# Low parts of the weights in three buffers, an own single buffer for the modulation vectors' tiles, and the mixer's parameters loaded later, in a hybrid diffusion layer on one core

## The chip, the cores and the metric

The kernel runs on one core of a Trainium2 chip. The time is that of the device in microseconds (us); the time before is the median of three runs. Engines are named as in the profile: PE is TensorE's matmul side and PEld its weight loads, DVE is VectorE, ACT is ScalarE, POOL is GpSimd, and SP is SyncE, whose queue (SPq) issues all of this kernel's DMAs. Every engine takes its instructions in the order in which the program lists them; an instruction that waits for a semaphore holds back all that is listed behind it on the same engine.

## The reference

One layer over 256 latent tokens and 256 context tokens of width 2048, in float32. Two conditioning vectors (`c` and `c_ctx`) give six modulation vectors each; the latent tokens use all six, the context tokens only the first two.

```python
mod = (silu_c @ w_mod[l] + b_mod[l])[:, None, :]
sh1, sc1, g1, sh2, sc2, g2 = jnp.split(mod, N_MOD, axis=-1)
h = modulate(rms_norm(x, norm_w[l, 0]), sh1, sc1)          # the same for ctx: hc
y, yc = token_mixers(h, hc, w_in[l], ..., w_out[l], ctx_out)
x = x + g1 * rms_norm(y, norm_w[l, 1])
h2 = modulate(rms_norm(x, norm_w[l, 2]), sh2, sc2)
x = x + g2 * rms_norm(conv_ffn(h2, ffn_up[l], ffn_conv_w[l], ffn_conv_b[l], ffn_down[l], True),
                      norm_w[l, 3])
```

`token_mixers` projects with `w_in` into seven parts, runs a gated linear recurrence in eight heads in both directions beside a convolution of width 31, and projects the two results with `w_out`. `conv_ffn` projects up to 2 x 5632 columns, convolves the gate half 3x3 on a grid, multiplies `gelu(gate)` with the other half and projects down.

## The kernel before

Every weight matrix is streamed through SBUF in tiles of 128 x 2048 float32 (1 MB). For full precision each tile is split: ACT casts it to the high part `whi` (L137), DVE subtracts to get the low part `wlo` (L140), and PE makes three products in place of one (high x high, high x low, low x high; L197 to L199 and L206 to L208). The raw tile is `raw`. Weight tiles are numbered here in the order in which they are used: 0 to 39 are five per head (ff, fb, q, b, a), 40 to 47 are g, 48 to 63 the output projection, 64 to 151 the up projection (gate and val in turn), 152 to 195 the down projection.

Four modulation vectors of the latent tokens (numbers 2 to 5 of the code) are not made on PE. Each is a sum over 16 tiles `graw` of 1 MB. DVE multiplies a tile with a column of the conditioning vector and adds it into an accumulator (L711 for the first tile of a vector, L713 for the others, two halves of 1024 columns a tile). Then `mod_cols` turns the accumulator by four groups of PE transposes `gT` (L727), and ACT sums them into columns (L730). The vector tiles are numbered 0 to 63 here: 0 to 15 are vector 2, 16 to 31 vector 3, 32 to 47 vector 4, 48 to 63 vector 5. One accumulator (`big`) serves vectors 2, 3 and 4.

The stages are: `phase0` (norm, first two modulation vectors, v projection), eight heads with `head_gemm` and `conv_gemm`, the g projections, `phase2` (output projection, residual, second norm), `phase3` (up projection with the grid convolution) and `phase4` (down projection). From the first head on, weight tiles are prepared ahead of their matmuls (`take`, `stage`).

What sets the order: a scheduler lists the instructions of each engine by readiness and priority. PE is held to the order of the code from the heads on (`self.order({ET.PE})`), so the place of the `gT` transposes between the matmuls is fixed by the code: `gemv` issues a vector's tiles at fixed places, and a count of PE time (`tick`) places the transposes about 5 us of matmuls behind the last tile. Splits of weight tiles have a raised priority (600), the sums of vector tiles a lowered one in the heads (-1000, `gemv_prio`) and none from the end of the heads on. Buffers come from pools: a tag with n buffers is a ring, in which tile k waits until tile k - n has been read for the last time. Before the change the rings are `raw` 3, `whi` 3 and `wlo` 2, and a vector tile takes its turn in the ring `raw` among the weight tiles, so that a weight tile can be loaded only when the vector tile ahead of it in the ring has been summed up. All DMAs stand in one queue on SP.

Of the kernel before, what the change touches and what calls it, by code (L numbers as in the profile page):

```python
# [8 lines left out]
F32 = mybir.dt.float32  # L9
# [6 lines left out]
P = 128  # L16
# [41 lines left out]
    ("lnw", HEADS),  # L58
    ("lnb", HEADS),
    ("hgw", 1),  # L60
    ("fcw", NFF * 9),
    ("fcb", NFF),
]
_POFF = {}
_n = 0
for _name, _w in _PCOLS:
    _POFF[_name] = (_n, _n + _w)
    _n += _w
NPAR = _n


def _ap(t, off, dims):
# [41 lines left out]
class _Kernel:  # L114
# [15 lines left out]
    def wtile(self, i, prio=600, hi=None, lo=None):  # L130

        src, (oh, ol) = self.srcs[i], self.places[i]
        raw = self.raws.pop(0) if self.raws else self.raw_tile(src, prio)
        with self.tc.high_priority(prio):
            if hi is None:
                hi = self.stg.tile([P, WBUF], F32R, tag="whi", name="whi", bufs=3)[:, oh:oh + 2048]
            self.nc.scalar.copy(hi, raw)  # L137
            if lo is None:
                lo = self.stg.tile([P, WBUF], F32R, tag="wlo", name="wlo", bufs=2)[:, ol:ol + 2048]
            self.nc.vector.tensor_sub(lo, raw, hi.bitcast(F32))  # L140
        return hi, lo

# [79 lines left out]

    def par(self, name, i=0, n=1):
        o = _POFF[name][0]
        return self.params[:, o + i:o + i + n]

    def rsqrt(self, out, t):

# [12 lines left out]
    def run(self):  # L241
# [90 lines left out]
        self.hid_hi = hid.tile([P, NFF, SEQ], F32R, name="hid_hi")  # L332
        self.hid_lo = hid.tile([P, NFF, SEQ], F32R, name="hid_lo")
        upp, up = enter(name="up", bufs=2, side="right")
        self.phase3(up)
        leave(upp)
        leave(h2p)
# [11 lines left out]
    def consts(self):  # L349
        nc, a, cst = self.nc, self.a, self.cst  # L350
        self.params = cst.tile([P, NPAR], F32, name="params")
        nc.sync.dma_start(self.params, a["params"])
        self.ident = cst.tile([P, P], F32, name="ident")
        self.masks = cst.tile([P, 5, 32], U8, name="masks")
        self.onecol = cst.tile([P, 1], F32, name="onecol")
        nc.gpsimd.memset(self.onecol, 1.0)
        self.mhalf = cst.tile([P, 2], F32, name="mhalf")
        nc.gpsimd.memset(self.mhalf, -0.5)


# [24 lines left out]
        self.oml = cst.tile([P, n], F32, name="oml")  # L385
        nc.vector.tensor_scalar(self.oml, self.lb, -1.0, 1.0, op0=ALU.mult, op1=ALU.add)


        o = _POFF["cT"][0]
        cc = self.params[:, o:o + 2 * KB]  # L390
        self.cs = cst.tile([P, 2 * KB], F32, name="cs")
        nc.scalar.activation(self.cs, cc, AF.Sigmoid)
        nc.vector.tensor_mul(self.cs, cc, self.cs)

        self.bsc1 = cst.tile([P, KB], F32, name="bsc1")
        nc.vector.tensor_scalar_add(self.bsc1, self.par("bmod", KB, KB), 1.0)
        self.ab = cst.tile([P, 2, KB, 2], F32, name="ab")
        self.mc = cst.tile([P, 4, KB], F32, name="mc")

    def late_consts(self):  # L400
        self.nc.sync.dma_start(self.ident, self.a["ident"])
# [9 lines left out]
    def phase0(self, p0, px, srcs):  # L411
# [49 lines left out]
        def gemv_row(q, t):  # L461

            if t == 0:
                rows[q] = px.tile([P, 512], F32, tag="row", name="row", bufs=P0_ROW)
            tag, n = (("raw", 3), ("whi", 3), ("wlo", 2), ("raw", 3), ("whi", 3), ("wlo", 2), ("raw", 3), ("whi", 3))[self.nt % 8]
            self.nt += 1
            w = self.stg.tile([P, 2048 if tag == "raw" else WBUF], F32, tag=tag, name="mraw", bufs=n)[:, 0:2048]
            nc.sync.dma_start(w, a["wm1"][q, t])
            for g in range(4):
                nc.tensor.matmul(rows[q][g * 32:(g + 1) * 32, :], cz[:, t * 4 + g, :], w[:, g * 512:(g + 1) * 512],  # L470
# [228 lines left out]

    def gemv_tile(self, s, kb):  # L700
        nc = self.nc
        w = self.stg.tile([P, 2048], F32, tag="raw", name="graw", bufs=3)
        nc.sync.dma_start(w, self.a["wm2"][s - 2, kb])
        c = self.cs[:, kb:kb + 1]
        if kb == 0:
# [524 lines left out]
def _pack(inputs):  # L1230
# [25 lines left out]
        "fcw": inputs["ffn_conv_w"][0].reshape(9, NFF, P).transpose(2, 1, 0).reshape(P, -1),  # L1256
        "fcb": _cols(inputs["ffn_conv_b"][0]),
    }
    a["params"] = np.ascontiguousarray(np.concatenate([parts[n] for n, _ in _PCOLS], axis=1))
    i = np.arange(P)  # L1260
    a["ident"] = np.eye(P, dtype=np.float32)
    a["masks"] = np.ascontiguousarray(np.stack(
# [3 lines left out]


# [11 lines left out]
```

## Time and profile before

| what | before |
|---|---|
| median of three runs | 1421.55 us (1419.74 to 1441.67) |
| profiled execution | 1419.87 us, of which the span from first to last instruction is 1418.1 us |
| PE busy | 1375.5 us (97%) |
| DVE busy | 1073.3 us (76%) |
| ACT busy | 716.6 us (51%) |
| DMA | 329.38 MB, mean 232 GB/s |
| mean granted TensorE clock | 0.995 |

Busy time is the time in which an engine had at least one instruction under way. Of the span, PE was idle for 1418.1 - 1375.5 = 42.6 us. A row of the timeline gives start, length, engine, line, operation, tiles and count, and in brackets the idle time ahead of it with what ended it. A row of the waits gives the sum in us, how many there were and the longest.

### The profile page before, as it was taken

The numbers are of one execution on the slowest core, as the hardware profiler recorded it, in microseconds if no ns is written. First come the engines' busy times: TensorE is split into PE (matmuls) and PEld (weight loads), VectorE is DVE, ScalarE is ACT, GpSimd is POOL, SyncE is SP. The second block draws the span as 40 slices with busy tenths as digits, with TensorE's granted clock in tenths as the row PEclk, the third lists the DMA queues.
The fourth block names the chain that finished last, engine by engine and source line by source line (L and its number), as shares of the span: only waits on it lengthen the run. The fifth ranks groups of instructions, "written<-read, shape, count | busy, mean of one in ns | idle before, by whom it ended". The sixth has DMA issues, their size and how long they took to land.

```text
span 1418.1 us, 24793 instructions
## 1 busy us (share of the span) xinstructions
PE 1375.5 (97%) x10272; PEld 1224.9 (86%) x10272; DVE 1073.3 (76%) x1577; ACT 716.6 (51%) x1174; POOL 31.2 (2%) x57
## 2 busy tenths in 40 slices
PE   4999999999999999999999999999999999999997
PEld 2566888888888898988999999999999998888886
DVE  4444788999999899777788788778878886767544
ACT  4333456666656665536744444454545443333532
POOL 0000001001000011000000000000000000000000
PEclk9999999999999999999999999999999999999999
DMA  9988676446645565788355555555555558878652
GB/s 374 391 325 330 258 267 218 160 188 238 222 167 207 208 226 189 286 305 302 123 205 180 205 185 203 181 206 189 199 184 203 193 194 340 312 287 306 242 187 106
DMA packets 49153, 329.38 MB, mean 232 GB/s; under 512 B 5392, under 2 KB 5648, under 8 KB 10896
## 3 DMA queue, kind: packets, MB, share of 16 engines
q1 hardware_dynamic: 49040, 327.80, 62.7%
q8 instruction: 80, 1.31, 0.4%
q14 instruction: 33, 0.27, 0.1%
HBM read 323.58 MB, written 4.19 MB: 231 GB/s over the span
## 4 chain that ended last, share of the span: by engine, by line
PE 77%; DVE 11%; ACT 4%; DMA 3%; issue 2%; POOL 2%; SPq 0%; DVEq 0%; POOLq 0%; ACTq 0%
PE val L197 6%; PE val L199 6%; PE val L198 6%; PE dn L206 6%; PE gate L197 6%; PE dn L208 6%; PE gate L199 5%; PE dn L207 5%; PE gate L198 5%; DVE wlo L140 3%; DVE acc L930 3%; PE v L206 2%; PE wo L208 2%; PE wo L206 2%; PE wo L207 2%
## 5 line engine op out<-in xcount | busy, mean ns | idle before, releaser
L137 ACT CAST whi<-raw 128x2048 fp32r<-128x2048 f32 x193 | 368.9, 1912 | 371.3 <-PE val L198 120.1
L140 DVE TENSOR_TENSOR wlo<-raw,whi 128x2048 fp32r<-128x2048 f32 x193 | 441.9, 2289 | 149.4 <-PE dn L207 59.7
L199 PE MATMUL val<-h,wlo 128*128 128x256 f32 x704 | 194.3, 276 | 0.0
L197 PE MATMUL val<-h,whi 128*128 128x256 f32 x704 | 194.3, 276 | 0.0
L198 PE MATMUL val<-h,whi 128*128 128x256 f32 x704 | 194.3, 276 | 0.0
L197 PE MATMUL gate<-h,whi 128*128 128x256 f32 x688 | 189.9, 276 | 0.0
L198 PE MATMUL gate<-h,whi 128*128 128x256 f32 x688 | 189.9, 276 | 0.0
L199 PE MATMUL gate<-h,wlo 128*128 128x256 f32 x688 | 189.9, 276 | 0.0
L1139 DVE SCALAR_TENSOR_TENSOR gacc<-gate,params,gacc 128x189 f32<-128x189 f32 (+2 forms) x352 | 152.4, 433 | 23.3 <-ACT gacc L1133 12.5
L206 PE MATMUL dn<-whi,hid_hi 128*128 128x512 f32 x352 | 137.4, 390 | 0.0
L208 PE MATMUL dn<-whi,hid_lo 128*128 128x512 f32 x352 | 137.0, 389 | 0.0
L207 PE MATMUL dn<-wlo,hid_hi 128*128 128x512 f32 x352 | 136.9, 389 | 0.0
L197 PEld LDWEIGHTS val<-h,whi 128*128 128x128 f32 x704 | 132.2, 188 | 0.0
L198 PEld LDWEIGHTS val<-h,whi 128*128 128x128 f32 x704 | 132.2, 188 | 0.0
L199 PEld LDWEIGHTS val<-h,wlo 128*128 128x128 f32 x704 | 132.1, 188 | 0.0
L199 PEld LDWEIGHTS gate<-h,wlo 128*128 128x128 f32 x688 | 129.2, 188 | 0.0
L197 PEld LDWEIGHTS gate<-h,whi 128*128 128x128 f32 x688 | 129.1, 188 | 0.0
L198 PEld LDWEIGHTS gate<-h,whi 128*128 128x128 f32 x688 | 129.1, 188 | 0.0
L713 DVE SCALAR_TENSOR_TENSOR big<-graw,cs,big 128x1024 f32<-128x1024 f32 x90 | 113.5, 1278 | 14.0 <-DMA graw<-in_wm_dram 13.9
L930 DVE SCALAR_TENSOR_TENSOR acc<-u,params,acc 128x242 f32<-128x242 f32 (+14 forms) x240 | 98.8, 472 | 0.0
L208 PEld LDWEIGHTS dn<-whi,hid_lo 128*128 128x128 f32 x352 | 66.1, 188 | 13.9
L207 PEld LDWEIGHTS dn<-wlo,hid_hi 128*128 128x128 f32 x352 | 66.1, 188 | 13.5
(270 smaller groups left out, 2681.4 us busy)
## 6 DMA issues: line engine op xcount, KB each, us to landing
raw<-in_wup_dram SPq DMA_DIRECT2D x88, 1024.0 KB, 4.8
graw<-in_wm_dram SPq DMA_DIRECT2D x64, 1024.0 KB, 5.0
raw<-in_win_dram SPq DMA_DIRECT2D x48, 1024.0 KB, 5.0
raw<-in_wdn_dram SPq DMA_DIRECT2D x44, 1024.0 KB, 4.9
mraw<-in_wm_dram SPq DMA_DIRECT2D x32, 1024.0 KB, 9.6
raw<-in_wout_dram SPq DMA_DIRECT2D x16, 1024.0 KB, 4.9
vraw<-in_wv_dram SPq DMA_DIRECT2D x16, 512.0 KB, 6.2
x<-in_x_dram SPq DMA_DIRECT2D x2, 1024.0 KB, 7.1
```

Source lines behind the costliest of these rows:

```text
L137: self.nc.scalar.copy(hi, raw)
L140: self.nc.vector.tensor_sub(lo, raw, hi.bitcast(F32))
L197: nc.tensor.matmul(out, wh, xh, start=start, stop=False)
L198: nc.tensor.matmul(out, wh, xl, start=False, stop=False)
L199: nc.tensor.matmul(out, wl, xh, start=False, stop=stop)
L206: nc.tensor.matmul(out, xh, wh, start=start, stop=False)
L207: nc.tensor.matmul(out, xh, wl, start=False, stop=False)
L208: nc.tensor.matmul(out, xl, wh, start=False, stop=stop)
L713: nc.vector.scalar_tensor_tensor(self.gacc[:, sl], w[:, sl], c, self.gacc[:, sl], op0=ALU.mult, op1=ALU.add)
L930: nc.vector.scalar_tensor_tensor(d, u[:, lo + o:hi + o], self.par("cw", j * CONVW + k), d, op0=ALU.mult, op1=ALU.add)
L1139: nc.vector.scalar_tensor_tensor(o, g[:, r0 + dy:r1 + dy, c0 + dx:c1 + dx], self.par("fcw", j * 9 + (dy + 1) * 3 + dx + 1), o, op0=ALU.mul ...
```

## The change

Three things are edited. The ring `wlo` has three buffers in place of two. Vector tiles `graw` no longer take their turn in the ring `raw`; they have a ring of their own with one buffer. The tiles `mraw` of the first stage, which go round the rings of the stream that is not yet running, use the ten buffers of all four rings. Room comes from a smaller scratch for DMA descriptors, and from the parameters: those of the grid convolution (`fcw`, `fcb`, 440 of the 921 columns) become a tensor of their own, `fparams`, which is loaded at the start of `phase3`. A tile `pad` of 56 columns that nothing uses is put behind the constants.

```diff
@@ parameters
+]
+
+_FCOLS = [
     ("fcw", NFF * 9),
     ("fcb", NFF),
 ]
@@ wtile
-                lo = self.stg.tile([P, WBUF], F32R, tag="wlo", name="wlo", bufs=2)[:, ol:ol + 2048]
+                lo = self.stg.tile([P, WBUF], F32R, tag="wlo", name="wlo", bufs=3)[:, ol:ol + 2048]
@@ par
         o = _POFF[name][0]
-        return self.params[:, o + i:o + i + n]
+        t = self.fparams if name in ("fcw", "fcb") else self.params
+        return t[:, o + i:o + i + n]
@@ run, ahead of phase3
         upp, up = enter(name="up", bufs=2, side="right")
+        self.fparams = up.tile([P, NFCP], F32, name="fparams", bufs=1)
+        nc.sync.dma_start(self.fparams, a["fparams"])
         self.phase3(up)
@@ consts
+        cst.tile([P, 56], F32, name="pad")
@@ gemv_row
-            tag, n = (("raw", 3), ("whi", 3), ("wlo", 2), ("raw", 3), ("whi", 3), ("wlo", 2), ("raw", 3), ("whi", 3))[self.nt % 8]
+            tag, n = (("raw", 3), ("whi", 3), ("wlo", 3), ("raw", 3), ("whi", 3), ("wlo", 3), ("graw", 1), ("raw", 3),
+                      ("whi", 3), ("wlo", 3))[self.nt % 10]
@@ gemv_tile
-        w = self.stg.tile([P, 2048], F32, tag="raw", name="graw", bufs=3)
+        w = self.stg.tile([P, 2048], F32, tag="graw", name="graw", bufs=1)
         nc.sync.dma_start(w, self.a["wm2"][s - 2, kb])
@@ kernel
-    nc = bacc.Bacc("TRN2", target_bir_lowering=False, num_devices=1)
+    nc = bacc.Bacc("TRN2", target_bir_lowering=False, num_devices=1, dynamic_dma_scratch_size=1024)
```

The lines of the kernel move by 5 to 12: L140, L703, L713, L727 before are L145, L714, L724, L738 after. PE's rows stay in the same order from end to end. Those of DVE and SP move, since the scheduler orders them by when buffers come free. The rows below leave out nothing between the first and the last of each piece; `x11` means that the row stands eleven times in a row.

The first place is DVE in the third head, around the end of the convolution of the head before it, where the sum of vector 2 ends. `acc` is the convolution's accumulator, `big` that of the vector, `ss` belongs to the readout. Before:

```order
L930 SCALAR_TENSOR_TENSOR acc<-u,params,acc 128x241
L933 TENSOR_TENSOR acc<-acc 128x256
L711 TENSOR_SCALAR big_101<-graw,cs 128x1024
L713 SCALAR_TENSOR_TENSOR big_101<-graw,cs,big_101 128x1024
L898 TENSOR_SCALAR ss<-ss 128x2
L140 TENSOR_TENSOR wlo<-raw,whi 128x2048
```

After:

```order
L941 SCALAR_TENSOR_TENSOR acc<-u,params,acc 128x241
L724 SCALAR_TENSOR_TENSOR big_102<-graw,cs,big_102 128x1024
L944 TENSOR_TENSOR acc<-acc 128x256
L724 SCALAR_TENSOR_TENSOR big_102<-graw,cs,big_102 128x1024 x11
L722 TENSOR_SCALAR big_102<-graw,cs 128x1024
L909 TENSOR_SCALAR ss<-ss 128x2
L145 TENSOR_TENSOR wlo<-raw,whi 128x2048
```

Before, all 16 tiles of vector 2 are summed ahead of this place, and the next row that reads `graw` (L711) opens vector 3. After, the halves of tile 10 stand around the row L944, and those of tiles 11 to 15 behind it in one block. At the same place in the sixth head, where vector 3 ends, the block has nine rows: the second half of tile 27 and tiles 28 to 31.

The second is SP's queue at the same place. Before, weight tile 7 to weight tile 14:

```order
L127 DMA raw<-in_win_dram 128x2048 x2
L703 DMA graw<-in_wm_dram 128x2048
L127 DMA raw<-in_win_dram 128x2048
L703 DMA graw<-in_wm_dram 128x2048
L127 DMA raw<-in_win_dram 128x2048 x2
L703 DMA graw<-in_wm_dram 128x2048
L127 DMA raw<-in_win_dram 128x2048 x2
L703 DMA graw<-in_wm_dram 128x2048 x2
L127 DMA raw<-in_win_dram 128x2048
```

After, weight tile 12 to weight tile 17:

```order
L132 DMA raw<-in_win_dram 128x2048
L714 DMA graw<-in_wm_dram 128x2048
L132 DMA raw<-in_win_dram 128x2048 x2
L714 DMA graw<-in_wm_dram 128x2048
L132 DMA raw<-in_win_dram 128x2048 x2
L714 DMA graw<-in_wm_dram 128x2048 x6
L132 DMA raw<-in_win_dram 128x2048
```

Before, vector tile 15, the last of vector 2, is issued between weight tiles 11 and 12. After, it is the fifth of the six that stand between weight tiles 16 and 17. Vector tile 10 is the one ahead of weight tiles 15 and 16.

The third place is DVE near the end of `phase2`, where vector 4 ends. `h` and `wroom` are rooms for low parts that lie outside the ring, `Y` and `part` belong to the residual, and L732 and L743 are the first rows that read the finished columns. Before:

```order
L713 SCALAR_TENSOR_TENSOR big_101<-graw,cs,big_101 128x1024 x2
L140 TENSOR_TENSOR h_6190<-raw,h_6190 128x2048 x2
L1007 TENSOR_TENSOR Y<-wo,G 128x512 x2
L1027 TENSOR_REDUCE part_6643<-ss_6199 128x2
L140 TENSOR_TENSOR wlo<-raw,whi 128x2048
L1028 TENSOR_SCALAR part_6643<-part_6643 128x2
L140 TENSOR_TENSOR wroom<-raw,wroom 128x2048
L140 TENSOR_TENSOR wlo<-raw,whi 128x2048
L732 TENSOR_TENSOR mc<-mc,params 128x16
```

After:

```order
L145 TENSOR_TENSOR wroom<-raw,wroom 128x2048
L1018 TENSOR_TENSOR Y<-wo,G 128x512 x2
L1038 TENSOR_REDUCE part_6644<-ss_6200 128x2
L145 TENSOR_TENSOR wlo<-raw,whi 128x2048
L1039 TENSOR_SCALAR part_6644<-part_6644 128x2
L145 TENSOR_TENSOR wlo<-raw,whi 128x2048
L724 SCALAR_TENSOR_TENSOR big_102<-graw,cs,big_102 128x1024 x4
L743 TENSOR_TENSOR mc<-mc,params 128x16
```

Before, vector tile 47 is summed ahead of the rows `Y` (the first row of the piece). After, tiles 46 and 47 are summed behind them and behind weight tiles 64 and 65; in SP's queue tile 46 stands behind weight tile 66 and tile 47 behind weight tile 68. In `phase4`, where vector 5 ends, the last two halves (tile 63) stand behind the low part of weight tile 181 before, and behind that of weight tile 184 after.

More of the change, by code (lines that the diff above doesn't have):

```diff
@@ L64 @@
 _POFF = {}
[L65 to L69, printed above, removed]
+for _list in (_PCOLS, _FCOLS):
+    _n = 0
+    for _name, _w in _list:
+        _POFF[_name] = (_n, _n + _w)
+        _n += _w
+NPAR = sum(_w for _, _w in _PCOLS)
+NFCP = sum(_w for _, _w in _FCOLS)
 def _ap(t, off, dims):
@@ L464, in gemv_row @@
                 rows[q] = px.tile([P, 512], F32, tag="row", name="row", bufs=P0_ROW)
-            tag, n = (("raw", 3), ("whi", 3), ("wlo", 2), ("raw", 3), ("whi", 3), ("wlo", 2), ("raw", 3), ("whi", 3))[self.nt % 8]
+            tag, n = (("raw", 3), ("whi", 3), ("wlo", 3), ("raw", 3), ("whi", 3), ("wlo", 3), ("graw", 1), ("raw", 3),
+                      ("whi", 3), ("wlo", 3))[self.nt % 10]
             self.nt += 1
-            w = self.stg.tile([P, 2048 if tag == "raw" else WBUF], F32, tag=tag, name="mraw", bufs=n)[:, 0:2048]
+            w = self.stg.tile([P, WBUF if tag[0] == "w" else 2048], F32, tag=tag, name="mraw", bufs=n)[:, 0:2048]
             nc.sync.dma_start(w, a["wm1"][q, t])
@@ L1258, in _pack @@
     }
-    a["params"] = np.ascontiguousarray(np.concatenate([parts[n] for n, _ in _PCOLS], axis=1))
+    for name, cols in (("params", _PCOLS), ("fparams", _FCOLS)):
+        a[name] = np.ascontiguousarray(np.concatenate([parts[n] for n, _ in cols], axis=1))
     i = np.arange(P)
```

## The prediction

> **What bounds the kernel now.** First the page's line of busy times, then a table of the stages, cut where PE's matmuls change name (first stage to 158.9, heads and g to 586.4, output projection to 688.3, up projection to 1167.3, down projection with vector 5 to 1344.9, and the rest), and PEld's waits for low parts.
>
> ```profile
> span 1418.1 us, 24793 instructions
> PE 1375.5 (97%) x10272; PEld 1224.9 (86%) x10272; DVE 1073.3 (76%) x1577; ACT 716.6 (51%) x1174; POOL 31.2 (2%) x57
> ```
>
> ```profile
> core 0: us, PE busy (x) PEld busy (x) DVE busy (x) ACT busy (x) POOL busy (x), PEclk, DMA share, GB/s
> 0.00:60.00 60.00, 39.71 (x208) 20.95 (x209) 26.39 (x74) 25.56 (x48) 3.45 (x11) 0.94 0.99 391
> 60.00:158.90 98.90, 97.94 (x531) 67.37 (x529) 53.25 (x81) 37.27 (x56) 0.31 (x1) 1.00 0.80 309
> 158.90:586.40 427.50, 415.44 (x3745) 372.67 (x3745) 386.01 (x716) 270.18 (x602) 23.75 (x39) 1.00 0.59 215
> 586.40:688.30 101.90, 100.28 (x484) 83.96 (x483) 73.17 (x74) 56.95 (x105) 2.59 (x4) 1.00 0.75 278
> 688.30:1167.30 479.00, 479.00 (x4225) 478.73 (x4224) 383.19 (x531) 234.17 (x270) 0.00 (x0) 1.00 0.54 191
> ```
>
> ```profile
> PEld ff L199 <- DVE wlo L140: 4.4, 5, 1.4
> ...
> PEld a L199 <- DVE wlo L140: 1.7, 3, 0.9
> ...
> PEld g L199 <- DVE wlo L140: 0.9, 1, 0.9
> ```
>
> PE is the bound nearly everywhere. It never idles in the up projection, where most of the weight tiles are split, and loses 427.5 - 415.4 = 12.1 us in the heads. A third low-part buffer can only take away waits for a low part, and those rows sum to 4.4 + 1.7 + 0.9 = 7.0 us. DVE is busy for 386 of 427.5 us in the heads (90%): there its order decides.
>
> **Part by part: the buffers.** The third buffer lets DVE prepare a tile earlier. I count -6 us, bounds 0 and -7.0.
>
> **The vector tiles.** With one buffer, tile k + 1 is issued when DVE has read both halves of tile k, and is summed when it has landed. The nearest rows are these of the chain of waits, where a vector tile was loaded right behind a sum, and the summary of its issues.
>
> ```profile
> 364.75 1.19 DVE big L713
> ...
> 365.97 4.97 DMA graw<-in_wm_dram
> ...
> 371.04 0.09 DVE big L713
> ```
>
> ```profile
> 1321.87 2.47 DVE L713 SCALAR_TENSOR_TENSOR gacc<-graw,cs,gacc 128x1024 f32<-128x1024 f32 x2
> ```
>
> ```profile
> graw<-in_wm_dram SPq DMA_DIRECT2D x64, 1024.0 KB, 5.0
> DMA to landing us min/median/max: 4.7/5.0/8.4
> ```
>
> From the issue to the start of the sum it takes 371.04 - 365.97 = 5.07 us, and two halves take 2.47. A tile that must wait for the one before it costs 5.07 + 2.47 = 7.54 us, whatever else is idle. That matters only where somebody waits. In the heads DVE's sums have the lowest priority, and no weight tile waits for them any more, so the scheduler lets them slide. Before, tile 15's rows stand ahead of the end of the second head's convolution; after, five tiles are left when PE, in its fixed order, reaches the transposes. That is the block of eleven rows, and PE can do nothing behind the first `gT` until tile 15's first half is in. These rows of the timeline show when PE gets there and when DVE, in the same place, has done the convolution.
>
> ```profile
> 259.63 0.65 PE L837 MATMUL cr<-Q,x 128*32 128x128 f32 x16
> ...
> 263.52 0.39 PE L199 MATMUL fb<-hT,wlo 128*128 128x512 f32 x1
> 263.75 0.60 PE L727 MATMUL gT<-ident,big 128*128 128x128 f32 x4
> ```
>
> ```profile
> 264.22 0.22 DVE L850 COPY_PREDICATED diag<-masks,lv 128x64 f32<-128x64 uint8 x1
> ...
> 267.11 4.33 DVE L930 SCALAR_TENSOR_TENSOR acc<-u,params,acc 128x251 f32<-128x251 f32 x11
> 271.47 0.42 DVE L933 TENSOR_TENSOR acc<-acc 128x256 f32<-128x256 f32 x1
> ```
>
> First block: the taps end at 267.11 + 4.33 = 271.44; tile 10's halves and the add between them take 2.47 + 0.42 more, so tile 11 can be issued at 274.3. The copies at 264.22 read what the recurrence's matmuls write, which end at 260.3, so all of this can be at most 3.9 us earlier: 270.4. I take the middle, 272.3. PE wants the columns at 263.75, so 8.6 us have gone before the block begins. Then come four tiles of 7.54 (11 to 14) and of tile 15 the load and one half, 5.07 + 1.24 = 6.3: together 8.6 + 30.2 + 6.3 = 45.1 us of PE, bounds 43.2 and 47.1.
>
> ```profile
> 453.48 0.60 PE L727 MATMUL gT<-ident,big 128*128 128x128 f32 x4
> ```
>
> ```profile
> 455.22 4.32 DVE L930 SCALAR_TENSOR_TENSOR acc<-u,params,acc 128x251 f32<-128x251 f32 x11
> ```
>
> Second block (vector 3): the taps end at 459.54, tile 27 at 462.4, and with the same middle at 460.4, which is 6.9 us behind PE. Then three tiles of 7.54 (28 to 30) and 6.3 for tile 31: 6.9 + 22.6 + 6.3 = 35.8 us, bounds 34 and 38.
>
> ```profile
> 651.77 0.60 PE L727 MATMUL gT<-ident,big 128*128 128x128 f32 x4
> ```
>
> ```profile
> 652.78 1.28 DVE L1007 TENSOR_TENSOR Y<-wo,G 128x512 f32<-128x512 f32 x2
> 653.98 0.15 DVE L1027 TENSOR_REDUCE part<-ss 128x2 f32<-128x6 f32 x1
> 654.55 2.29 DVE L140 TENSOR_TENSOR wlo<-raw,whi 128x2048 fp32r<-128x2048 f32 x1 [0.43 <-ACT whi L137]
> ...
> 657.65 2.29 DVE L140 TENSOR_TENSOR wroom<-raw,wroom 128x2048 fp32r<-128x2048 f32 x1 [0.73 <-ACT wroom L137]
> ```
>
> Third, in `phase2` (vector 4): here no row shows the new order, so the price has two ends. If the room's low part (`wroom`) is done before the rows `Y`, DVE runs from 652.78: `Y`, `part`, two weight tiles and tile 46 are 1.28 + 0.15 + 2 x 2.29 + 2.47, to 661.3; tile 47 is issued only then, 6.3 more, 667.6: 15.8 us behind PE. If `wroom` comes as late as in the row above, 659.9, tile 46 is issued only there (it stands in SP's queue behind weight tile 66, which takes over that raw buffer): 659.9 + 7.54 + 6.3 = 673.7, 22 us. I take 16, since three buffers let the weight tiles come earlier.
>
> ```profile
> 1330.51 0.60 PE L727 MATMUL gT<-ident,gacc 128*128 128x128 f32 x4
> ```
>
> ```profile
> 1330.54 2.29 DVE L140 TENSOR_TENSOR wlo<-raw,whi 128x2048 fp32r<-128x2048 f32 x1 [2.72 <-PE dn L207]
> ```
>
> Fourth, in `phase4` (vector 5): with three buffers the low part of tile 184 is released by the matmuls that end at 1330.5, as that of 183 in the row above was with two, and tile 63 is summed behind it: 2.29 + 1.24 = 3.5 us of PE, bounds 0 and 5.
>
> ```profile
> 541.00:547.00 6.00, 2.72 (x150) 2.14 (x149) 6.00 (x12) 3.23 (x7) 0.20 (x2) 1.00 0.49 178
> 547.00:550.40 3.40, 3.40 (x17) 3.40 (x17) 3.40 (x11) 1.09 (x4) 0.00 (x0) 0.50 0.77 294
> ```
>
> Behind an idle stretch the clock is lower. PE idles for 6.0 - 2.72 = 3.3 us in the first of these windows, and the granted clock is 0.50 for the next 3.4 us: 1.7 us of work lost. Four stretches of that kind make 6.8 us (bounds 3.4, if only long ones count once or twice, and 14, if it takes two such times to come back). The Trainium skill, "TensorE: Matmul & The Clock Gate", Part 1, "What's actually happening", says the same of any idle window of about 3.4 us, and that one busy window restores the clock; by that rule the stretch of 45 us would cost no more than the one of 3.5.
>
> The Trainium skill, "Trainium Kernel Development and Optimization", section "Best Practices", asks to double-buffer so that DMA overlaps compute, which speaks against a single buffer. Taken as a price for every vector tile, the rule would give 64 x 4.97 = 318 us. By the rows only the eleven loads named above (11 to 15, 28 to 31, 46, 47) stand between PE and its columns; behind the others PE has matmuls to do.
>
> **The parameters.** The start is bound by DMA (391 GB/s in the first 60 us, with PE idle for 20 of them), and the first load shrinks from 921 to 481 columns, 225 KB.
>
> ```profile
> params<-in_params_dram SPq DMA_DIRECT2D x1, 460.5 KB, 3.4
> ```
>
> ```profile
> 681.72 0.33 SPq L1105 DMA_DIRECT2D x1d<-x  x1
> ```
>
> At 391 GB/s that is -0.6 us. The new load `fparams` is issued behind the second `x1d`, at 681.7 us, and needed when the first gate tile is multiplied, 48 matmuls of 479.0 / 4225 = 0.113 us behind 688.3, 5.4 us; at 3.4 us it is hidden, and without that cover it would cost at most 3.4. The ten buffers of the first stage change nothing that I can see: PE is busy for 97.9 of the 98.9 us from 60 to 158.9. They stand at 0.
>
> **Sum.** 45.1 + 35.8 + 16 + 3.5 + 6.8 - 6 - 0.6 = +100.6 us. The profiled execution took 1419.87 us, 1.7 below the median of the runs (1421.55), so the forecast is 1419.9 + 100.6 = 1520.5, 1521 us.
>
> **Rivals.** (1) *No wait at the transposes.* The order is only a list; if DVE ran so far ahead of PE that the blocks were over when PE came, the change would give what the buffers are worth: 1420 - 7 = 1413 us. For it: before, PE never waited for an accumulator. Against it: the block stands behind taps that themselves stand behind matmuls which PE does 4 us ahead of `gT`, so DVE can't be earlier than 260.3. It decides for this if the block's loads are issued ahead of their sums, which one buffer excludes. 6%. (2) *Faster by over 2%.* All of PE's idle time is 42.6 us, and 28 would have to go; the waits that the buffers can end are 7. 1%. (3) *Smaller blocks.* If a lone load landed at the rate of the start (1 MB at 391 GB/s, 2.7 us) in place of 4.97, a tile would take 5.2 us: 11 loads x 2.3 = 25 us less, 1496. The minimum of 64 landings, 4.7, speaks against it. 7%. (4) *The blocks starve the weights too.* SP's queue is blocked with DVE, and weight tiles 17 and 37 stand behind the last vector tile of a block. PE has tiles 12 and 13 ready. In DVE's order 14 stands behind the readout's row `ss`, and PE reads it in `a`:
>
> ```profile
> 274.86 0.17 DVE L898 TENSOR_SCALAR ss<-ss 128x2 f32<-128x2 f32 x1 [0.98 <-ACT on L896]
> ```
>
> ```profile
> 287.24 0.28 PE L197 MATMUL a<-hT,whi 128*128 128x256 f32 x1
> ```
>
> That is 11.1 us and 23.5 us behind `gT`. If this slack went, a load, DVE's half of a split and as much again for ACT's (4.97 + 2 x 2.29 = 9.6 us) would be added at two places: 1540. 10%.
>
> **Chances and range.** The forecast has 76%, the rivals 6, 1, 7 and 10. A measurement of this kernel tells about 2% from no change, 28 us here: faster 1%, within 2% 6%, slower 93%. The forecast's own bounds are 43.2 + 34 + 12 + 0 + 3.4 - 7 - 0.6 = +85 and 47.1 + 38 + 22 + 5 + 14 - 0 - 0.6 = +125.5; the third term's lower end is set at 12 by judgement, below the 15.8 worked out. With rivals 3 and 4 the range is 1490 to 1548.
>
> **What would show it.** Right: four idle stretches of PE that end in L738 with DVE's L724 as releaser, of about 45, 36, 16 and 3.5 us; nine loads of `graw` about 7.5 us apart in the first two; the granted clock at 0.50 behind each; no wait for `wlo` worth over 1 us in the heads; the up projection at 479 us as before. Wrong: `gT` without a wait, or loads in the blocks that come closer than 7 us, or a stretch that ends in a weight tile's L204 or L212.

## The result and the profile after

The changed kernel takes 1529.36 us (median of four runs, 1525.48 to 1534.39), the kernel before 1420.64 us on the same chip: a ratio of 1.076, with a 95% interval of 1.072 to 1.081. The times of the kernel before lie in two groups, near 1421 and near 1439 us, and the ratios to it below are taken over both. The forecast of 1521 us is 8 us under the median and 4 under the profiled execution (1525.48 us). The profile's page, span and busy times:

```profile
span 1523.4 us, 24833 instructions
PE 1380.9 (91%) x10272; PEld 1230.5 (81%) x10272; DVE 1068.4 (70%) x1577; ACT 719.8 (47%) x1174; POOL 22.4 (1%) x57
```

PE is busy for 5 us more than before and idle for 1523.4 - 1380.9 = 142.5 us, where it was 42.6. The table of the stages of the changed kernel, cut at the same matmuls, says where (start and end, length, the busy times of PE, PEld, DVE, ACT and POOL, the granted clock, DMA share and GB/s); below it the row of before for the down projection, which stands in no table so far:

```profile
60.00:160.66 100.66, 99.70 (x543) 68.93 (x541) 53.16 (x80) 39.85 (x58) 0.31 (x1) 1.00 0.82 318
160.66:664.31 503.65, 414.80 (x3744) 375.19 (x3745) 383.81 (x714) 266.63 (x598) 14.93 (x39) 0.92 0.51 181
664.31:786.20 121.89, 101.69 (x483) 84.84 (x482) 78.03 (x78) 57.35 (x107) 2.59 (x4) 0.93 0.67 248
786.20:1265.47 479.27, 479.27 (x4228) 479.00 (x4226) 377.87 (x528) 238.75 (x271) 0.00 (x0) 1.00 0.55 190
1265.47:1450.17 184.70, 179.15 (x802) 148.30 (x801) 116.27 (x78) 70.37 (x75) 0.00 (x0) 0.99 0.76 282
```

```profile
1167.30:1344.90 177.60, 177.60 (x802) 147.28 (x801) 116.63 (x76) 70.18 (x75) 0.00 (x0) 1.00 0.79 299
```

The start has become longer by 160.66 - 158.90 = 1.8 us, the heads with g by 503.65 - 427.50 = 76.2, the stage of the output projection by 121.89 - 101.90 = 20.0, the up projection by 0.3 and the down projection by 184.70 - 177.60 = 7.1. That is 105.4 us, and the spans differ by 105.3. PE's timeline has, ahead of the first transposes of each vector, the idle time in brackets (the rows between these four are left out):

```profile
307.56 1.09 PE L738 MATMUL gT<-ident,big 128*128 128x128 f32 x4 [44.74 <-DVE big L724]
529.54 1.09 PE L738 MATMUL gT<-ident,big 128*128 128x128 f32 x4 [37.02 <-DVE big L724]
747.89 1.09 PE L738 MATMUL gT<-ident,big 128*128 128x128 f32 x4 [18.00 <-DVE big L724]
1434.41 1.09 PE L738 MATMUL gT<-ident,gacc 128*128 128x128 f32 x4 [5.55 <-issue]
```

Four stretches, 44.74 + 37.02 + 18.00 + 5.55 = 105.3 us in sum. The fourth bears the name `issue` in place of `L724`, as if PE had waited for nothing; DVE's rows, shown further down, have the first half of tile 63 end just ahead of it, as in the other three. In the first stretch DVE's timeline reads, from the end of the convolution on:

```profile
263.94 4.32 DVE L941 SCALAR_TENSOR_TENSOR acc<-u,params,acc 128x251 f32<-128x251 f32 x11
268.18 1.27 DVE L724 SCALAR_TENSOR_TENSOR big<-graw,cs,big 128x1024 f32<-128x1024 f32 x1
269.38 0.41 DVE L944 TENSOR_TENSOR acc<-acc 128x256 f32<-128x256 f32 x1
269.71 1.27 DVE L724 SCALAR_TENSOR_TENSOR big<-graw,cs,big 128x1024 f32<-128x1024 f32 x1
275.93 2.48 DVE L724 SCALAR_TENSOR_TENSOR big<-graw,cs,big 128x1024 f32<-128x1024 f32 x2 [4.94 <-DMA graw<-in_wm_dram]
283.35 2.48 DVE L724 SCALAR_TENSOR_TENSOR big<-graw,cs,big 128x1024 f32<-128x1024 f32 x2 [4.95 <-DMA graw<-in_wm_dram]
290.66 2.48 DVE L724 SCALAR_TENSOR_TENSOR big<-graw,cs,big 128x1024 f32<-128x1024 f32 x2 [4.83 <-DMA graw<-in_wm_dram]
298.76 2.48 DVE L724 SCALAR_TENSOR_TENSOR big<-graw,cs,big 128x1024 f32<-128x1024 f32 x2 [5.62 <-DMA graw<-in_wm_dram]
306.13 2.48 DVE L724 SCALAR_TENSOR_TENSOR big<-graw,cs,big 128x1024 f32<-128x1024 f32 x2 [4.89 <-DMA graw<-in_wm_dram]
```

DVE does nothing here but wait for one tile, sum it, and wait for the next, whose load could not begin before. The sums start 7.4, 7.3, 8.1 and 7.4 us apart. PE is released 1.4 us into the last of them, by its first half. In the second stretch the four sums of tiles 28 to 31 start at 505.88, 513.30, 520.71 and 528.11 us, 7.4 apart.

### The profile page after: what moved, and what is told of

It is laid out like the page before. It is cut to its first block, busy times and chain, and to the rows that moved or that the text cites. A ratio compares the mean times of both kernels' runs of the same rounds, so it can differ in the third digit from the quotient of the medians.

```text
span 1523.4 us, 24833 instructions
## 1 busy us (share of the span) xinstructions
PE 1380.9 (91%) x10272; PEld 1230.5 (81%) x10272; DVE 1068.4 (70%) x1577; ACT 719.8 (47%) x1174; POOL 22.4 (1%) x57
## 4 chain that ended last, share of the span: by engine, by line
PE 75%; DVE 12%; DMA 6%; ACT 4%; issue 3%; POOL 1%; SPq 0%; DVEq 0%; POOLq 0%; ACTq 0%
PE val L202 5%; PE val L204 5%; PE val L203 5%; PE dn L211 5%; PE dn L212 5%; PE dn L213 5%; PE gate L202 5%; PE gate L204 5%; PE gate L203 5%; DMA graw<-in_wm_dram 4%; DVE wlo L145 3%; DVE big L724 3%; DVE acc L941 2%; PE v L211 2%; PE v L213 2%
## 5 line engine op out<-in xcount | busy, mean ns | idle before, releaser
L145 DVE TENSOR_TENSOR wlo<-raw,whi 128x2048 fp32r<-128x2048 f32 x193 | 441.5, 2288 | 176.1 <-ACT whi L142 176.0
L724 DVE SCALAR_TENSOR_TENSOR big<-graw,cs,big 128x1024 f32<-128x1024 f32 x90 | 113.5, 1278 | 74.0 <-DMA graw<-in_wm_dram 74.0
L1150 DVE SCALAR_TENSOR_TENSOR gacc<-gate,fparams,gacc 128x189 f32<-128x189 f32 (+2 forms) x352 | 151.9, 432 | 10.9
L941 DVE SCALAR_TENSOR_TENSOR acc<-u,params,acc 128x241 f32<-128x241 f32 (+14 forms) x240 | 99.2, 468 | 0.0
L738 PE MATMUL gT<-ident,big 128*128 128x128 f32 x48 | 8.7, 311 | 99.8 <-DVE big L724 99.8
L738 PEld LDWEIGHTS gT<-ident,big 128*128 128x128 f32 x48 | 6.5, 160 | 101.6 <-issue 100.9
```

What stands on the lines that cost most here:

```text
L724: nc.vector.scalar_tensor_tensor(self.gacc[:, sl], w[:, sl], c, self.gacc[:, sl], op0=ALU.mult, op1=ALU.add)
L738: nc.tensor.transpose(ps[:, j * P:(j + 1) * P], gacc[:, kb * P:(kb + 1) * P], self.ident)
L941: nc.vector.scalar_tensor_tensor(d, u[:, lo + o:hi + o], self.par("cw", j * CONVW + k), d, op0=ALU.mult, op1=ALU.add)
L1150: nc.vector.scalar_tensor_tensor(o, g[:, r0 + dy:r1 + dy, c0 + dx:c1 + dx], self.par("fcw", j * 9 + (dy + 1) * 3 + dx + 1), o, op0=ALU.mul ...
```

## The experiments

Theory: a ring of one buffer makes load and sum of the vector tiles take turns, and the low priority lets the scheduler leave four or five of them to the place where PE needs the result. Rivals: the third low-part buffer or the new rings upset the order by themselves; any ring of their own gets into DVE's way; the low priority alone is to blame. The diffs are against the changed kernel. Where a run changes the rings, the list of rings that `mraw` goes round in the first stage is changed with them; these lines are left out.

**The vector tiles back in the shared ring.** Low parts keep three buffers and the parameters stay split.

```diff
-        w = self.stg.tile([P, 2048], F32, tag="graw", name="graw", bufs=1)
+        w = self.stg.tile([P, 2048], F32, tag="raw", name="graw", bufs=3)
```

> The changed kernel with the vector tiles back in the ring raw (three buffers, shared with the weight tiles); the low parts keep three buffers, the parameters stay split. Theory (the loss is all the vector tiles' own single buffer): no wait at the transposes gT, no wait for low parts in the heads, so the gain of the third buffer alone shows: about 9 us below the kernel before, 1411 us. Rival A (the third low-part buffer reorders DVE and is the cause): 1500 us or more. Rival B (the new order of loads costs by itself): 1421 us or above, without the 9 us.

Measured: 1429.45 us (1427.45 to 1446.75, ten runs), a ratio to before of 1.003 (0.998 to 1.009). No `gT` waits for a sum, so the loss goes with the ring of the vector tiles. The gain that I expected of the third low-part buffer did not come; the time is the one that rival B names. From PE's waits in this kernel:

```profile
PE cT L975 <- ACT un L970: 6.4, 3, 3.4
PE cr L848 <- ACT Q L833: 5.6, 2, 2.8
...
PE a L204 <- DVE wlo L145: 0.4, 1, 0.4
PE ff L204 <- DVE wlo L145: 0.3, 1, 0.3
```

The waits for low parts in the heads are all but gone, 0.7 us, and 12 us of waits for the convolution (`un`) and the recurrence (`Q`) stand in their place. This profiled execution took 1438.90 us, 9.5 above the median, with the heads 8.5 us and the stage of the output projection 8.8 us longer than before; which of its waits the shorter runs have too is not known.

**Two low-part buffers, and the single buffer for vector tiles kept.**

```diff
-                lo = self.stg.tile([P, WBUF], F32R, tag="wlo", name="wlo", bufs=3)[:, ol:ol + 2048]
+                lo = self.stg.tile([P, WBUF], F32R, tag="wlo", name="wlo", bufs=2)[:, ol:ol + 2048]
```

> The changed kernel with two low-part buffers again; the vector tiles keep their own single buffer. Theory: the blocks of eleven and nine rows are still in DVE's order, so four waits at gT of about 45, 37, 17 and 5 us and none of the third buffer's gain: about 1533 us, 4 to 9 us above the changed kernel. Rival A (the third low-part buffer is the cause): 1421 us. Rival C (both parts are needed for the loss): between 1440 and 1500 us.

Measured: 1525.03 us (1523.44 to 1527.99), ratio 1.069 (1.059 to 1.078). The third low-part buffer has no part in the loss. Its gain, for which I had put this kernel 4 to 9 us above the changed one, is not there either. PE's rows of the first three waits (the rows between are left out):

```profile
304.98 1.09 PE L738 MATMUL gT<-ident,big 128*128 128x128 f32 x4 [42.92 <-DVE big L724]
524.82 1.09 PE L738 MATMUL gT<-ident,big 128*128 128x128 f32 x4 [34.97 <-DVE big L724]
748.04 1.09 PE L738 MATMUL gT<-ident,big 128*128 128x128 f32 x4 [24.63 <-DVE big L724]
```

The third wait is 6.6 us longer than with three buffers, near the upper end of that term (22 us) and in its way: tile 46 is issued only 8 us behind PE's arrival, and it lands 7.9 us later.

**Priority 0 in place of -1000 for the sums in the heads.** One buffer for vector tiles and three for low parts, as in the change.

```diff
-        self.gemv_prio = -1000
+        self.gemv_prio = 0
```

> The changed kernel with the vector tiles' sums at priority 0 in the heads in place of -1000; one buffer as in the changed kernel. Theory (one buffer costs only where the sums are put off until PE waits): the block of eleven rows shrinks to the two rows of tile 15 behind the convolution's taps, that of nine goes; waits at gT of about 9, 0, 8 and 5.6 us: about 1439 us. Rival D (a single buffer costs its load time whatever the order): above 1500 us.

Measured: 1460.27 us (1459.00 to 1463.43), ratio 1.023 (1.014 to 1.032). From PE's waits:

```profile
PE gT L738 <- DVE big L724: 23.9, 2, 13.7
...
PE gT L738 <- issue: 5.6, 1, 5.6
```

With the same single buffer, 69 us of the loss are gone once the sums are not put off. What is left, 39 us over the lower group of before, is 29.5 at `gT` (the 5.6 of the fourth vector among them) and small waits; I had expected 22.6 at `gT` and few others, so 1439 us was missed by 21.

**Two half buffers.** The room of one vector tile holds two buffers of 1024 columns, and each half of a tile is a load of 512 KB. The sums, whose lines are left out, read `ws[i]` in place of `w[:, sl]`.

```diff
-        w = self.stg.tile([P, 2048], F32, tag="graw", name="graw", bufs=1)
-        nc.sync.dma_start(w, self.a["wm2"][s - 2, kb])
+        ws = []
+        for i in range(GEMV_N):
+            w = self.stg.tile([P, D // GEMV_N], F32, tag="graw", name="graw", bufs=GEMV_N)
+            nc.sync.dma_start(w, self.a["wm2"][s - 2, kb][:, i * D // GEMV_N:(i + 1) * D // GEMV_N])
+            ws.append(w)
```

> The changed kernel with the same room for vector tiles cut into two buffers of half a tile (1024 columns, 512 KB), each half loaded by itself; priority -1000 as in the changed kernel. Theory: the load of one half runs beside the sum of the other, the scheduler keeps up, and only the first place has a block (five halves behind the taps, three of them loaded there): a wait at gT of about 13 us, none at the other three, and the 9 us of the third buffer gained: about 1425 us. Rival E (the priority alone makes the blocks, however many buffers): 1500 us or more.

Measured: 1489.49 us (1470.96 to 1490.22), ratio 1.040 (1.029 to 1.052). Of the profiled execution (1488.88), 18.6 us lie in the pace of the up projection, which the kernel before shows too in some of its runs (below); the run of 1470.96 fits one without them. So the halves cost some 51 us over before, where I had expected 5. From PE's waits, and the summary of the loads of `graw`:

```profile
PE cT L978 <- ACT un L973: 20.6, 6, 4.7
PE gT L741 <- DVE big L727: 15.2, 1, 15.2
```

```profile
  DMA graw<-in_wm_dram: 96.8, 56
...
DMA to landing us min/median/max: 3.6/5.4/9.3
```

The one wait at `gT` is near the expected 13. What the theory missed is that a load of half a tile does not hide behind the sum of the other half, which takes 1.28 us: the load took 3.6 us at the least, against 4.7 for a whole tile, and 5.4 in the median, against 5.6 in the changed kernel (many halves are issued two at a time, so the median is not that of a lone half). DVE, which takes its list in order, was stopped 56 times, for 96.8 us. The longest wait at `cT`, 4.67 us in the second head, follows two such stops, of 2.22 and 0.98 us, that stand in DVE's list ahead of the convolution's norm; that the other waits at `cT` come from such stops too was not followed.

**Two whole buffers for the vector tiles, two for low parts.** The same room, used the other way round.

```diff
-                lo = self.stg.tile([P, WBUF], F32R, tag="wlo", name="wlo", bufs=3)[:, ol:ol + 2048]
+                lo = self.stg.tile([P, WBUF], F32R, tag="wlo", name="wlo", bufs=2)[:, ol:ol + 2048]
-        w = self.stg.tile([P, 2048], F32, tag="graw", name="graw", bufs=1)
+        w = self.stg.tile([P, 2048], F32, tag="graw", name="graw", bufs=2)
```

> The room of the third low-part buffer goes to a second buffer of the vector tiles' own ring; low parts have two again, as before the change. Theory (one buffer is the cost, because a load can only be issued when DVE has read the tile before): with two, a load runs beside the sum of the tile before it, no block of tiles stands ahead of a transpose, and gT waits for less than 3 us; about 1425 us. Rival A (a ring of their own puts loads into DVE's way however many buffers it has, as the two half buffers did): gT without a wait but cT behind un about 20 us, 1470 us. Rival B (low priority alone makes the blocks): gT waits of 20 us and more, 1500 us.

Measured: 1425.89 us (1422.62 to 1430.46, ten runs), ratio 0.999 (0.994 to 1.003). No wait at `gT`, at the low priority of -1000. Against the kernel with one such buffer and two for low parts (1525.03) the second buffer is worth 99 us. The summary of the loads of `graw`, DVE's idle time ahead of the sums and how often:

```profile
  DMA graw<-in_wm_dram: 18.2, 10
```

The same row of the changed kernel:

```profile
  DMA graw<-in_wm_dram: 104.2, 29
```

So neither a ring of their own nor the priority alone makes the loss; it takes the single buffer, and the priority decides how much of it falls on PE. Against the lower group of before, 1421.24 us beside this run, the kernel is still 4.7 us slower.

**The parameters alone.** Low parts have two buffers and vector tiles share the raw ring, as before; the parameters are split, the scratch is small, and `pad` is there.

```diff
-                lo = self.stg.tile([P, WBUF], F32R, tag="wlo", name="wlo", bufs=3)[:, ol:ol + 2048]
+                lo = self.stg.tile([P, WBUF], F32R, tag="wlo", name="wlo", bufs=2)[:, ol:ol + 2048]
-        w = self.stg.tile([P, 2048], F32, tag="graw", name="graw", bufs=1)
+        w = self.stg.tile([P, 2048], F32, tag="raw", name="graw", bufs=3)
```

> Only the mixer's parameters are loaded later, with the smaller scratch; low parts have two buffers and the vector tiles share the raw ring, as before the change. Theory of the prediction: -0.6 us, 1419 us. Rival: in the profiles of the changed kernel and of the one with the shared ring the first matmul of ff came 1.7 us later than before; if the split of the parameters does that, this kernel shows ff at 160.6 instead of 158.9 us and takes about 1422 us; if ff stays at 158.9, the ten or nine buffers of the first stage did it.

Measured: 1422.35 us (1419.52 to 1437.73, ten runs), ratio 0.995 (0.990 to 1.000). PE's first row of `ff` of before, and of this kernel:

```profile
158.90 0.50 PE L197 MATMUL ff<-hT,whi 128*128 128x512 f32 x1 [0.68 <-ACT v L686]
```

```profile
160.49 0.50 PE L202 MATMUL ff<-hT,whi 128*128 128x512 f32 x1 [0.68 <-ACT v L696]
```

The start is 1.6 us later with the smaller first load, not 0.6 earlier. That is the rival of this run, in both its numbers. All kernels with the split began `ff` later in their profiles than before, by 0.6 to 3.3 us (the half buffers by 7.1), where a second profile of before differs from the first by 0.4. On SP's queue the issue of `ident`, one of the first loads, is longer: 0.92 us in this kernel and 1.38 in the changed one, against 0.58 before. That does not explain it here, since the loads ahead of `ident` are issued faster: the second `x` is issued at 6.67 us, against 6.76 before. Whether the smaller scratch makes the start longer, or the place of the tiles, was not tried; it is worth about 0.1%.

**A fourth raw buffer.** As the kernel above, with four buffers in the ring `raw`, which weight tiles and vector tiles share.

```diff
-            raw = self.stg.tile([P, 2048], F32, tag="raw", name="raw", bufs=3)
+            raw = self.stg.tile([P, 2048], F32, tag="raw", name="raw", bufs=4)
-                lo = self.stg.tile([P, WBUF], F32R, tag="wlo", name="wlo", bufs=3)[:, ol:ol + 2048]
+                lo = self.stg.tile([P, WBUF], F32R, tag="wlo", name="wlo", bufs=2)[:, ol:ol + 2048]
-        w = self.stg.tile([P, 2048], F32, tag="graw", name="graw", bufs=1)
+        w = self.stg.tile([P, 2048], F32, tag="raw", name="graw", bufs=4)
```

> The room goes to a fourth raw buffer, which weight tiles and vector tiles share; low parts have two. Theory: loads can start earlier, but before the change PE waited for few loads, so 1418 us (1414 to 1424), with the 7 us of waits for low parts as before. Rival: another number of buffers moves the order on DVE, and small waits come in at the convolution and the recurrence as in the kernel with the shared ring and three low-part buffers, 1430 us.

Measured: 1417.52 us (1416.44 to 1421.02, ten runs), ratio 0.992 (0.988 to 0.996). It beats both kernels, though most of the 0.8% comes from the two groups of before's times; against the median of the lower group, 1421.24 us, it is 0.3%. Of the 25 runs of before beside it ten lie in the upper group, of its own ten none; whether the buffer has a part in that is not shown.

**Priority 700 for the sums everywhere,** ahead of the splits of weights (600). One buffer for vector tiles, three for low parts.

```diff
-        self.gemv_prio = -1000
+        self.gemv_prio = 700
-        self.gemv_prio = 0
+        self.gemv_prio = 700
```

> As the changed kernel (one buffer for vector tiles, three for low parts), with the sums of the vector tiles at priority 700 instead of -1000, ahead of DVE's other work in all stages. Theory (putting the sums off is most of the loss, and one buffer is harmless when the sums come early): no wait at gT in the heads, about 1440 us. Rival (each lone tile then blocks DVE for a load of about 5 us, ahead of low parts and convolution): gT without a wait in the heads, but DVE idle for graw well over 100 us, PE waits at cT and for wlo, 1500 us or more.

Measured: 1477.62 us (1475.53 to 1479.89), ratio 1.033 (1.023 to 1.043). Both views missed. `gT` waits nowhere, and DVE is idle for `graw` for only 25.8 us, but its other work is late for PE. Four rows of PE's waits:

```profile
PE ct L957 <- DVE acc L944: 10.9, 3, 3.6
PE cx L889 <- DVE diag L861: 10.4, 3, 5.9
PE cT L975 <- ACT un L970: 9.5, 6, 3.2
PE cr L848 <- ACT att L817: 9.1, 3, 3.2
```

In the heads, which take 485.5 us against 427.5 before, PE is idle for 48.5 us against 12.1 and busy for 437.0 against 415.4, at a granted clock of 0.94 against 1.00: many shorter waits lower the clock as well. So the waits at `gT` can be removed by order, and turn into waits at the convolution (`ct`, `cT`) and the recurrence (`cx`, `cr`). With one buffer, no order tried reached the time of two.

**Four raw buffers and three for low parts,** which fills the change's room.

```diff
-            raw = self.stg.tile([P, 2048], F32, tag="raw", name="raw", bufs=3)
+            raw = self.stg.tile([P, 2048], F32, tag="raw", name="raw", bufs=4)
-        w = self.stg.tile([P, 2048], F32, tag="graw", name="graw", bufs=1)
+        w = self.stg.tile([P, 2048], F32, tag="raw", name="graw", bufs=4)
```

> The whole room of the change, used otherwise: raw has four buffers, which weight tiles and vector tiles share, and low parts have three. Theory (raw buffers are what the stream lacks, low parts are not): as the kernel with four raw buffers alone, 1417 us (1413 to 1421), without waits for low parts. Rival (a third low-part buffer moves low parts ahead of the convolution on DVE, as with three raw buffers): waits at cT and cr of 10 us together and more, 1427 us.

Measured: 1447.42 us (1437.99 to 1457.33), ratio 1.020 (1.013 to 1.026); the profiled execution took 1440.91. The longest row of PE's waits in the heads:

```profile
PE cT L974 <- ACT un L969: 18.3, 9, 3.7
```

With two low-part buffers the same row has 5.7 us. No wait for a low part stands in PE's list any more, and the kernel is over 20 us slower than with two low-part buffers. Between the two profiles the heads differ by 21.6 us, of which 12.5 are idle time of PE and 9.1 busy time, at a granted clock of 0.97 against 1.00. The rival's waits came, and larger than I had put them, but its mechanism is not shown: at the first of them, which lasts 3.69 us, one low part stands ahead of the convolution's norm in both kernels, and what has come to stand ahead of it besides is half a vector tile.

**Five raw buffers, two for low parts.**

```diff
-            raw = self.stg.tile([P, 2048], F32, tag="raw", name="raw", bufs=3)
+            raw = self.stg.tile([P, 2048], F32, tag="raw", name="raw", bufs=5)
-                lo = self.stg.tile([P, WBUF], F32R, tag="wlo", name="wlo", bufs=3)[:, ol:ol + 2048]
+                lo = self.stg.tile([P, WBUF], F32R, tag="wlo", name="wlo", bufs=2)[:, ol:ol + 2048]
-        w = self.stg.tile([P, 2048], F32, tag="graw", name="graw", bufs=1)
+        w = self.stg.tile([P, 2048], F32, tag="raw", name="graw", bufs=5)
```

> The room goes to two more raw buffers, five in all, which weight tiles and vector tiles share; low parts have two. Theory (the fourth buffer has taken what loads cost): 1417 us, within 2 us of four buffers. Rival (each more buffer saves as much as the fourth seemed to): 1413 us.

Measured: 1417.63 us (1414.05 to 1418.75, seven runs), ratio 0.996 (0.992 to 0.999). The fifth buffer adds nothing to the fourth.

**The kernel before, once more.** No edit.

> The kernel before, once more, for its profile: its times lie in two groups, near 1420 and near 1439 us. If it falls into the upper group: by one view the up projection takes 497.5 us instead of 479.0, each matmul 117.5 ns behind the last in place of 113.4, as in the profile of the kernel with half buffers; by the other the 19 us lie in waits of PE or at a lower granted clock. If it falls into the lower group, it tells nothing.

Measured: 1437.15 us, in the upper group. The first view held. The rows of the up projection's `val` (least, median and most ns of one; first and last start), before and in this run:

```profile
L197 PE MATMUL val<-h,whi x704: 276/276/276, 694.0 to 1166.9; 128*128 128x256 f32 x176
```

```profile
L197 PE MATMUL val<-h,whi x704: 281/281/281, 692.7 to 1184.2; 128*128 128x256 f32 x176
```

From the first to the last it is 472.9 us in one and 491.5 in the other, 18.6 us, with PE busy throughout and the granted clock at 1.00 in both. The times differ by 17.3.

## Why the prediction was right, point by point

**The waits in the heads.** 45.1 us predicted for vector 2, 44.74 measured; 35.8 for vector 3, 37.02 measured. The working held in its parts too: the taps end at 263.94 + 4.32 = 268.26, and PE begins to wait at 307.56 - 44.74 = 262.82, so the taps end 5.4 us behind PE. I had worked with 272.3 for the issue of tile 11, 8.6 behind PE's 263.75; the trace has it at the end of the sum, 269.71 + 1.27 = 270.98, 8.2 behind. That start was the middle of two bounds and not read from a row, so the closeness is in part luck: in the second block, with the same middle, tile 28 is issued 8.5 us behind PE, where the working had 6.9. The cycle of a tile was 7.54 us in the working and 7.3 to 8.1 in the rows. All kernels with two or more whole buffers had no such wait.

**The third and fourth wait.** 16 predicted, 18.00 measured, of bounds 15.8 and 22. DVE's rows of that stage:

```profile
731.10 1.28 DVE L1018 TENSOR_TENSOR Y<-wo,G 128x512 f32<-128x512 f32 x2
...
738.42 2.48 DVE L724 SCALAR_TENSOR_TENSOR big<-graw,cs,big 128x1024 f32<-128x1024 f32 x2 [1.03 <-DMA graw<-in_wm_dram]
746.46 2.48 DVE L724 SCALAR_TENSOR_TENSOR big<-graw,cs,big 128x1024 f32<-128x1024 f32 x2 [5.56 <-DMA graw<-in_wm_dram]
```

It went by the lower end's order: `Y`, two weight tiles, tile 46, tile 47. What the term lacked is above all a wait of 1.03 us for tile 46 itself, and a load of tile 47 of 5.56 us in place of 5.07. The fourth wait was put at 3.5 (bounds 0 and 5) and took 5.55: the low part of tile 184 started not at PE's arrival (1434.41 - 5.55 = 1428.86) but at 1430.82, when ACT had made its high part. That term's mechanism, a low part and a half sum ahead of PE, was right and its start 2 us off.

```profile
1430.82 2.29 DVE L145 TENSOR_TENSOR wlo<-raw,whi 128x2048 fp32r<-128x2048 f32 x1 [3.13 <-ACT whi L142]
1433.03 2.47 DVE L724 SCALAR_TENSOR_TENSOR gacc<-graw,cs,gacc 128x1024 f32<-128x1024 f32 x2
```

**The clock.** Four times 1.7 us were predicted. Stretches of the changed kernel around the first wait, with the granted clock third from the end:

```profile
262.82:266.20 3.38, 0.00 (x1) 0.00 (x0) 3.38 (x10) 2.36 (x9) 0.00 (x0) 1.00 0.62 259
266.20:307.56 41.36, 0.00 (x0) 0.03 (x1) 16.14 (x19) 0.00 (x0) 0.00 (x0) 0.50 0.37 127
307.56:310.70 3.14, 3.14 (x10) 2.66 (x11) 1.05 (x1) 1.25 (x8) 0.00 (x0) 0.50 0.34 70
310.70:315.00 4.30, 4.30 (x24) 3.65 (x22) 0.00 (x0) 1.19 (x9) 0.00 (x0) 1.00 0.47 196
```

The clock falls 3.4 us into the idle time, stays down for all of it, and comes back 3.1 us after PE has resumed: 1.6 us lost. Behind the second and third wait it is at 0.50 for 3.1 us too, and behind the fourth, of 5.55 us, for some 2.7, 1.4 lost. The four make about 6, against 6.8. So a stretch of 44.74 us costs little more clock than one of 5.55. By the rule of the Trainium skill, "TensorE: Matmul & The Clock Gate", Part 1, "What's actually happening", one busy window brings the clock back; the trace agrees, with 2.7 to 3.1 us at each of the four. The price is not the same everywhere: in the kernel with four raw and three low-part buffers the clock stays at 0.50 for 5.1 us behind a wait of 3.69 us, 2.6 lost.

**The buffers, -6.** Here the size was near by luck and the cause was wrong. The heads became 76.2 us longer, with 44.74 + 37.02 + 2 x 1.6 = 85.0 of waits and clock, so the rest of them became 8.8 shorter, and PE's list has no wait for a low part any more. But the step said that the third low-part buffer does this. Its bound of 7.0 was read from PEld, too; PE's own waits for low parts before are 2.1 + 1.0 + 0.7 = 3.8 us. The heads of the kernel with two low-part buffers and the single vector buffer, in the table of its stages:

```profile
159.47:657.84 498.37, 413.60 (x3744) 374.21 (x3745) 384.45 (x713) 267.98 (x598) 26.39 (x39) 0.92 0.51 183
```

Of these 498.4 us 42.92 + 34.97 + 3.2 = 81.1 are waits and clock, so 417.3 remain, 10 less than before. So the third buffer is not needed for it. Either edit nearly ends PE's waits for low parts: 0.7 us are left with the third buffer and the shared ring, none with two low-part buffers and two vector buffers in their own ring. But in those two profiles the heads take 436.0 and 430.0 us, so neither makes them shorter by itself. In the kernels with the single buffer nine tiles are summed inside the waits that are taken off here, and whether the 8.8 us come from that stays open. The third low-part buffer alone, with vector tiles in the shared ring, made the kernel no faster than before (1429.45 against 1422.35 with two), and with four raw buffers the kernel with it was 20 us and more slower. Where it did help is the output projection: 18.00 against 24.63 us.

**The parameters, -0.6.** The start became longer instead, by 1.8 us here and 1.6 with the parameters alone. That step counted only the bytes of one load; what makes the start longer stays open. The load of `fparams` is hidden as predicted: no wait for it stands in PE's list, and the up projection takes 479.27 us.

**The sum.** +100.6 predicted, +105.6 measured between the profiled executions (1525.48 - 1419.87). The differences are +2.0 and +2.1 at the third and fourth wait, +0.9 at the first two, -0.8 at the clock, 2.4 at the start, and -2.8 in the rest of the heads; these make +3.8 of 5.0, and the rest are shares of under 0.5 us in the later stages. The median of the four runs lies 4 us above the profiled one: two runs took 1525.5 and 1525.7, two 1533.0 and 1534.4. No profile of the longer ones exists, and that stays open.

**The rivals.** (1), no wait: excluded by the four rows of PE. (2), faster: the best use found of the room gains 0.3% against before's lower group. (3), loads at the start's rate: the five loads of the first block kept DVE idle for 4.83 to 5.62 us. (4), starved weights: no wait for a part of a weight tile stands in PE's list of the changed kernel. The single buffer's price is 99 us against two, and not the 318 us that a price on each tile would give, since PE waited only at the last tiles of each vector. The rule that speaks against a single buffer (the Trainium skill, "Trainium Kernel Development and Optimization", "Best Practices", on double buffers) is borne out by that.

## What to carry to other kernels

A ring of one buffer makes load and use take turns, here 7.4 us a tile for 2.5 us of work. Where what reads the tiles is late by intention (a low priority on an engine that takes its list in order), count the tiles that are left when the next engine needs the result, and multiply. Price each edit of a bundle by itself: here the low-part buffer that was bought gained no time (1529.36 us with it, 1525.03 without), the room was worth a little as a fourth buffer of the ring that feeds everything, and removing waits at one place (three low-part buffers, sums ahead of all else, half tiles) mostly made waits at another.

## What the runs showed of the hardware

Half a tile (512 KB in rows of 4 KB) took at least 3.6 us from issue to landing, a whole one at least 4.7: half the bytes save about a quarter of the time of the fastest load. The medians, 5.4 us with the half buffers and 5.6 in the changed kernel, are not of lone loads: many halves are issued two at a time.

The clock that PE is granted can cost as much behind short waits as behind long ones: 2.6 us were lost behind an idle stretch of 3.69 us, and 1.6 behind one of 44.74.

The up projection's matmuls have two paces, with nothing of the program changed: 276 ns busy for one in most profiles and 281 in two (the kernel before once more, and the half buffers), which is 18.6 us over 4225 of them, at a granted clock of 1.00 in both. One pace holds for the whole stage. Before's times lie in two groups that far apart. What sets it was not found.
